# Issuing the first load of a SiLU-gate kernel as four transfers of every 8th, 4th and 2nd partition

## The chip, the cores and the metric

The kernel runs on one core of one Trainium2 chip. The metric is the device time of one execution in microseconds (us). Every run quoted here was fast, with a granted clock of 1.0. The page reckons with sixteen DMA engines (its queue lines give shares of 16 engines). Here they moved 134.22 MB from HBM into the kernel's tiles and 67.11 MB back. ACT (ScalarE) computes the SiLU and issues the loads, DVE (VectorE) does the product, and SP issues the stores.

## The reference

```python
def setup_inputs():
    batch, seq, dim = (32, 512, 2048)
    return {'x': np.random.randn(batch, seq, dim).astype(np.float32)}

def reference(x):
    half_dim = x.shape[-1] // 2
    x1, x2 = x[..., :half_dim].copy(), x[..., half_dim:].copy()
    silu_x1 = x1 * (1 / (1 + np.exp(-x1)))
    return (silu_x1 * x2).astype(np.float32)
```

134.22 MB are read and 67.11 MB are written. There is one SiLU and one product per output element, so the kernel is mostly transfer.

## The kernel before

The 16384 rows of x are cut into 16 tiles of 1024 rows. A tile is 8 MiB: 128 partitions, and in each of them 8 rows that are adjacent in HBM, which is 64 KiB. The input pool holds two tiles. A tile's store is one transfer of 4 MiB, but that of the last tile goes out in four pieces. The first load is moved ahead of the barrier at the program's start, so that it is under way as early as possible.

```python
    K = 8
    KC = 2
    PLAN = [K] * (num_rows // (P * K))
    in_pool = ctx.enter_context(tc.tile_pool(name="in_pool", bufs=2))
    out_pool = ctx.enter_context(tc.tile_pool(name="out_pool", bufs=2))
    # ... (view(flat, i) gives tile i's rows as p, k, d)
    nc.at_finalize(issue_ahead_of_the_first_barrier)   # moves the first DMA issue to before the barrier
    # ...
    def load(i):
        xt = in_pool.tile([P, K, in_cols], dt, name="xt")
        nc.scalar.dma_start(out=xt[:, :plan[i][1], :], in_=view(x_flat, i))
        loaded[i] = xt

    load(0)
    load(1)
    for i in range(n_tiles):
        # ...
        for c in range(0, k, KC):
            ce = min(c + KC, k)
            nc.scalar.activation(out=ot[:, c:ce, :], in_=xt[:, c:ce, :half],
                                 func=mybir.ActivationFunctionType.Silu)
            nc.vector.tensor_mul(out=ot[:, c:ce, :], in0=ot[:, c:ce, :], in1=xt[:, c:ce, half:])
            if last:
                nc.sync.dma_start(out=ov[:, c:ce, :], in_=ot[:, c:ce, :])
        if not last:
            nc.sync.dma_start(out=ov, in_=ot[:, :k, :])
        if i + 2 < n_tiles:
            load(i + 2)
```

## Time and profile before

| | before |
|---|---|
| time | 470.97 us (3 runs, 470.84 to 471.04) |
| span of the profiled run | 468.9 us |
| moved | 201.35 MB, mean 429 GB/s |
| DVE, ACT busy | 30%, 25% |

These lines are from the page of the kernel before. The GB/s line cuts the span into 40 slices of 11.7 us. The two queue lines give packets, MB and the packets' time as a share of sixteen engines' span; q10 carries the loads and q1 the stores. The last line gives the chain of waits as shares of the span.

```profile
DVE 142.3 (30%) x64; ACT 118.2 (25%) x65; POOL 0.2 (0%) x4
GB/s 431 375 447 403 447 447 447 403 419 431 447 447 403 447 492 363 442 492 391 458 403 439 456 447 403 409 442 447 447 403 444 467 386 447 442 419 481 400 409 354
q10 hardware_dynamic: 2304, 134.22, 66.4%
q1 hardware_dynamic: 2736, 67.11, 33.2%
DMA xt<-in_x_dram 80%; DVE ot L92 15%; ACT ot L87 3%; DVEq L128 0%
```

The two queues together fill 99.6% of the engines' span, from the first slice on. The compute engines are idle for most of it. The kernel is bound by its DMA engines, so work that is added to them anywhere is expected to show in the time.

Next is the timeline of the kernel before (start in us, duration, engine, line, operation; in brackets the idle time before it and what ended it).

```profile
0.13 1.13 ACTq L74 DMA_DIRECT2D xt<-in_x_dram  x2
1.29 1.28 ACT L87 ACT_TABLE_LOAD   x1 [1.29 <-PEq L117]
21.88 7.31 ACT L87 ACTIVATE ot<-xt 128x2048 f32<-128x2048 f32 x4 [19.31 <-DMA xt<-in_x_dram]
32.74 23.00 SPq L100 DMA_DIRECT2D out_dram<-ot  x2
44.54 7.31 ACT L87 ACTIVATE ot<-xt 128x2048 f32<-128x2048 f32 x4 [15.36 <-DMA xt<-in_x_dram]
```

Load 0 lands and releases the first activation at 21.88 us.

The stretches view counts each packet where it starts. For the first 12 us of the kernel before it gives (from:to and length in us, busy time of each engine, granted clock, DMA share, GB/s):

```profile
core 0: us, DVE busy (x) ACT busy (x) POOL busy (x), PEclk, DMA share, GB/s
0.00:4.00 4.00, 0.00 (x0) 1.28 (x1) 0.20 (x4) 1.00 0.76 262
4.00:12.00 8.00, 0.00 (x0) 0.00 (x0) 0.00 (x0) 1.00 1.21 524
```

A load packet is 64 KiB, one partition's share of a tile. 262 GB/s for 4 us is sixteen packets, 524 GB/s for 8 us is 64. The records do not name the engine of a packet. Each of the first sixteen in the order of start ends about when one of the next sixteen starts (4.37 us in the mean for both), so the k-th sixteen are called each engine's k-th packet here.

The single records behind this view give the finest reading. An engine's first packet takes 3.05 us in the mean, and each later one of load 0 takes 2.42 us in the mean, which is 27.1 GB/s for one engine.

### The profile page before, as it was taken

Reading aid. Unit: us, or ns where it says so; the run is one execution under the profiler, and the core shown is the slowest. Engines: PE = TensorE matmul, PEld = TensorE weight load, DVE = VectorE, ACT = ScalarE, POOL = GpSimd, SP = SyncE. Lnnn points to the kernel's source line nnn. Section 1 sums busy time; section 2 is a strip of 40 time slices with the busy share of each in tenths; the row PEclk is TensorE's granted clock in tenths of the full one; section 3 lists DMA queues with packets and bytes.
Section 4 is the critical chain, followed back from the end, with each engine's and each line's share of the span. In section 5 each row is a group of like instructions: output and inputs, shape, how many; then the busy total and the mean of one; then the engine's idle time right before and its main releaser. Section 6 shows DMA issues by size and latency. Waiting matters only on the chain.

```text
span 468.9 us, 269 instructions
## 1 busy us (share of the span) xinstructions
DVE 142.3 (30%) x64; ACT 118.2 (25%) x65; POOL 0.2 (0%) x4
## 2 busy tenths in 40 slices
DVE  0070705106061160601507025070250702407034
ACT  1142406023060330603206032060420604106051
POOL 0000000000000000000000000000000000000000
DMA  9899999999999998999999999999999989999998
GB/s 431 375 447 403 447 447 447 403 419 431 447 447 403 447 492 363 442 492 391 458 403 439 456 447 403 409 442 447 447 403 444 467 386 447 442 419 481 400 409 354
DMA packets 5042, 201.35 MB, mean 429 GB/s; under 512 B 560, under 2 KB 560, under 8 KB 560
## 3 DMA queue, kind: packets, MB, share of 16 engines
q10 hardware_dynamic: 2304, 134.22, 66.4%
q1 hardware_dynamic: 2736, 67.11, 33.2%
q14 instruction: 2, 0.02, 0.0%
HBM read 134.22 MB, written 67.11 MB: 429 GB/s over the span
## 4 chain that ended last, share of the span: by engine, by line
DMA 80%; DVE 15%; ACT 3%; DVEq 0%; issue 0%
DMA xt<-in_x_dram 80%; DVE ot L92 15%; ACT ot L87 3%; DVEq L128 0%
## 5 line engine op out<-in xcount | busy, mean ns | idle before, releaser
L92 DVE TENSOR_TENSOR ot<-ot,xt 128x2048 f32<-128x2048 f32 x64 | 142.3, 2286 | 319.5 <-ACT ot L87 319.5
L87 ACT ACTIVATE ot<-xt 128x2048 f32<-128x2048 f32 x64 | 116.9, 1897 | 338.8 <-DMA xt<-in_x_dram 338.8
L87 ACT ACT_TABLE_LOAD x1 | 1.3, 1283 | 1.3 <-PEq L117 1.3
L117 POOL MEMSET const-uint8-127<- 128x1 uint8 x1 | 0.1, 102 | 0.0
L117 POOL MEMSET const-bfloat16-1.0<- 128x1 bf16 x1 | 0.1, 101 | 0.0
L117 POOL MEMSET const-float32-0.0<- 128x1 f32 x1 | 0.1, 98 | 0.2 <-issue 0.2
L117 POOL MEMSET const-float32-1.0<- 128x1 f32 x1 | 0.1, 98 | 0.0
## 6 DMA issues: line engine op xcount, KB each, us to landing
out_dram<-ot SPq DMA_DIRECT2D x15, 4096.0 KB, 39.8
out_dram<-ot SPq DMA_DIRECT2D x4, 1024.0 KB, 5.7
xt<-in_x_dram ACTq DMA_DIRECT2D x16, 47.1
```

The source lines that it names most:

```text
L87: nc.scalar.activation(out=ot[:, c:ce, :], in_=xt[:, c:ce, :half], func=mybir.ActivationFunctionType.Silu,)
L92: nc.vector.tensor_mul(out=ot[:, c:ce, :], in0=ot[:, c:ce, :], in1=xt[:, c:ce, half:],)
L117: nc = _bacc.Bacc("TRN2", target_bir_lowering=False, num_devices=1)
```

## The change

The intent is a quicker start: the first transfer is small and covers every 8th partition, sixteen packets, and the transfers grow to 64 partitions. The first load alone is split. Stores stay whole, although they go through the same helper.

```diff
-def issue_ahead_of_the_first_barrier(nc):
+def issue_ahead_of_the_first_barrier(nc, count):
...
-    load = next(ins for ins in body.instructions if type(ins).__name__ == "InstDMACopy")
+    loads = [ins for ins in body.instructions if type(ins).__name__ == "InstDMACopy"][:count]
...
-    head.instructions = head.instructions[:at] + [load] + head.instructions[at:]
+    head.instructions = head.instructions[:at] + loads + head.instructions[at:]
...
+    STARTING = [slice(0, None, 8), slice(4, None, 8), slice(2, None, 4), slice(1, None, 2)]
...
-    nc.at_finalize(issue_ahead_of_the_first_barrier)
+    nc.at_finalize(lambda nc: issue_ahead_of_the_first_barrier(nc, len(STARTING)))
...
+    def start_ring(queue, dst, src, split):
+
+        for ps in STARTING if split else [slice(None)]:
+            queue.dma_start(out=dst[ps], in_=src[ps])
...
-        nc.scalar.dma_start(out=xt[:, :plan[i][1], :], in_=view(x_flat, i))
+        start_ring(nc.scalar, xt, view(x_flat, i), split=i == 0)
...
-            nc.sync.dma_start(out=ov, in_=ot[:, :k, :])
+            start_ring(nc.sync, ov, ot, split=False)
```

More of the change, by code (lines that the diff above doesn't have):

```diff
@@ L6 @@
 from concourse._compat import with_exitstack
-def issue_ahead_of_the_first_barrier(nc):
+def issue_ahead_of_the_first_barrier(nc, count):
     head, body = nc.main_func.blocks[:2]
-    load = next(ins for ins in body.instructions if type(ins).__name__ == "InstDMACopy")
+    loads = [ins for ins in body.instructions if type(ins).__name__ == "InstDMACopy"][:count]
     at = next(
         j for j, ins in enumerate(head.instructions)
-        if ins.engine == load.engine and type(ins).__name__ == "InstDrain"
+        if ins.engine == loads[0].engine and type(ins).__name__ == "InstDrain"
     )
-    body.instructions = [ins for ins in body.instructions if ins.name != load.name]
-    head.instructions = head.instructions[:at] + [load] + head.instructions[at:]
+    names = {ins.name for ins in loads}
+    body.instructions = [ins for ins in body.instructions if ins.name not in names]
+    head.instructions = head.instructions[:at] + loads + head.instructions[at:]
 @with_exitstack
```

## The prediction

> **What bounds the kernel now.** The DMA engines. On the page, load packets (66.4%) and store packets (33.2%) fill 99.6% of the sixteen engines' span of 468.9 us; DVE is busy 30%, ACT 25%. The chain of waits is 80% loads of xt. In the trace's DMA records every load packet is 64 KiB (one partition's row of a tile) and takes 2.418 us, 27.1 GB/s per engine, from each engine's second packet on. 201.35 MB at sixteen times that rate is 464.2 us (estimate), so only 4.7 us of the span are not transfer: 1.14 us before the first packet (in the stretches view no bytes in the first microsecond, sixteen packets start in the second), first packets of 3.0 to 3.4 us, two engines that start 0.6 us after the others, and the tail after the last load.
>
> **What the change does.** The first 8 MiB load becomes four issues. A DMA issue costs ACT 0.33 to 0.38 us, so three more are about 1 us; they delay load 1's issue and the activation table load, both of which have until about 20 us. No cost. The possible gain is a quicker start with a short first transfer: 0.1 to 0.3 us, since nothing before the first issue moves. 48 more completion packets of 9 ns, three per engine: nothing. Computation waits for the whole tile as before.
>
> **The cost I expect.** [...] So in the first two transfers [...] each 1 MiB should take about 4.84 us instead of 2.42. [...] Estimated loss: 2 x 2.42 = 4.84 us[...], less the start gain: 4 us net.
>
> **On the critical path?** Wholly. Load 1 is queued behind load 0 and the queues never run empty before the end, so transfer time lost at the start moves everything; nothing later takes it up.
>
> **Prediction.** 474.8 us, about 0.8% slower; 80% range 470.8 to 476.0. Chances: faster by over 2% 0.005, within 2% 0.955, slower by over 2% 0.04.
>
> **What would show it.** Load queue 2352 packets (2304 + 48). Each engine's first two packets take 4.5 to 5.3 us, the third onward 2.42. The first activation starts near 26 us instead of 21.88; all later steps come 4 us later at unchanged distances (58 us per two tiles). ACT and DVE busy unchanged.
>
> **What would make it wrong.** [...] Slow reads of rows 512 KiB apart would look alike[...].

Passages are cut from this text and from some of the expectations below, where the cuts are marked: they rested on statements of the hardware that no trace or run here shows. The sum of the forecast came to a loss of about 4 us: 2 x 2.42 = 4.84 us, less a term of 0.2 to 0.6 us, less the gain of 0.1 to 0.3 us at the start. The 2.42 us was measured in the kernel before. That the packets of the two 16-partition transfers take twice as long was the estimate; no trace had shown it then.

## The result, and the profile after

The changed kernel takes 475.0 us (6 runs, 474.89 to 475.18), beside 471.0 us for the kernel before (6 runs, 470.71 to 471.12). The ratio is 1.0086, with a 95% interval of 1.0073 to 1.0099. It is a slowdown of 0.9%, clear of noise but within 2%. Ratios in this document are the mean time of one kernel's fast runs over that of the other's fast runs of the same rounds, so they are not quite the ratio of the medians quoted.

The same lines of the page, for the changed kernel (slices of 11.8 us):

```profile
DVE 142.3 (30%) x64; ACT 118.2 (25%) x65; POOL 0.2 (0%) x4
GB/s 244 377 443 443 427 460 443 399 438 449 402 441 443 471 416 399 443 488 399 410 477 443 399 419 429 438 444 460 410 460 399 441 446 443 399 443 482 380 425 354
q10 hardware_dynamic: 2352, 134.22, 66.6%
q1 hardware_dynamic: 2736, 67.11, 32.9%
DMA xt<-in_x_dram 79%; DVE ot L101 15%; ACT ot L96 3%; DVEq L137 0%; ACTq L96 0%
```

Only the first slice stands out: 244 GB/s in place of 431. Compute is the same to the digit. The load queue has 48 packets more: in the DMA records it has 304 packets of 4 bytes in place of 256, of 9 ns each and sixteen to each transfer, and there are three transfers more.

The timeline and the first stretches of the changed kernel:

```profile
0.13 3.54 ACTq L77 DMA_DIRECT2D xt<-in_x_dram  x5
27.34 1.28 ACT L96 ACT_TABLE_LOAD   x1 [27.34 <-DMA xt<-in_x_dram]
28.63 7.31 ACT L96 ACTIVATE ot<-xt 128x2048 f32<-128x2048 f32 x4
39.50 20.77 SPq L77 DMA_DIRECT2D out_dram<-ot  x2
49.06 7.31 ACT L96 ACTIVATE ot<-xt 128x2048 f32<-128x2048 f32 x4 [13.12 <-DMA xt<-in_x_dram]
```

```profile
0.00:4.00 4.00, 0.00 (x0) 0.00 (x0) 0.20 (x4) 1.00 1.19 262
4.00:12.00 8.00, 0.00 (x0) 0.00 (x0) 0.00 (x0) 1.00 0.96 254
```

From 4 to 12 us the engines start two packets each (one of the 32 falls just outside) where they started four before. The DMA share stays near 1 (0.96): the engines are not waiting for work. Each of the first two packets simply takes about twice as long (4.77 and 4.95 us, below). Also, the activation table is now loaded after the wait for load 0 instead of at 1.29 us. The second tile's activation is 4.52 us late (49.06 against 44.54), and the span is 4.2 us longer (473.1 against 468.9).

The DMA records give the sixteen packets of each step of load 0, one per engine, as the mean in us:

| | before | changed |
|---|---|---|
| start of the first packet | 1.32 (1.14 to 1.84) | 1.76 (1.50 to 2.60) |
| 1st packet takes | 3.05 | 4.77 (4.24 to 5.27) |
| 2nd packet | 2.42 | 4.95 (4.95 to 4.96) |
| 3rd packet | 2.42 | 2.86 (2.60 to 3.13) |
| 4th to 8th packet, each | 2.42 | 2.42 |
| 8th packet ends | 21.28 | 26.43 |

The slow packets are the first two of each engine, the ones of the two 16-partition transfers. The sixteen of the first transfer are in flight together: the last starts at 2.60 us, and none has ended by then, since the shortest takes 4.24 us from 1.50 us at the earliest. (The steps here are the packets in order of their start, sixteen at a time.)

### The profile page after: what moved, and what is told of

It is laid out like the page before. It is cut to its first block, busy times and chain, and to the rows that moved or that the text cites. A ratio compares the mean times of both kernels' runs of the same rounds, so it can differ in the third digit from the quotient of the medians.

```text
span 473.1 us, 277 instructions
## 1 busy us (share of the span) xinstructions
DVE 142.3 (30%) x64; ACT 118.2 (25%) x65; POOL 0.2 (0%) x4
## 4 chain that ended last, share of the span: by engine, by line
DMA 79%; DVE 15%; ACT 3%; DVEq 0%; issue 0%; ACTq 0%
DMA xt<-in_x_dram 79%; DVE ot L101 15%; ACT ot L96 3%; DVEq L137 0%; ACTq L96 0%
```

## The experiments

The theory is that the set of partitions that a transfer writes sets the time of its packets; in the changed kernel it is 4.77 and 4.95 us for every 8th and 2.42 us for every 2nd. Why a set should be slow is not shown by any trace here. The theory's forecast is the one that stands before those of the rivals. The rivals are: several transfers or several issues cost by themselves; small transfers do; HBM rows that lie 512 KiB apart (every 8th partition, 64 KiB each) are slow to read; the queues are slow only while they start up. The first four runs share the kernel before at 470.78 us (9 runs), the next four at 470.92 us (11 runs), the last three at 470.86 us (7 runs).

### Three transfers of 32, 32 and 64 partitions

```diff
-    STARTING = [slice(0, None, 8), slice(4, None, 8), slice(2, None, 4), slice(1, None, 2)]
+    STARTING = [slice(0, None, 4), slice(2, None, 4), slice(1, None, 2)]
```

> First load as three transfers of every 4th and 2nd partition (32, 32, 64): the change without its two 16-partition transfers, [...] from each engine's second packet on 2.42 us; time 471.0 to 471.4 (the start may be 0.4 us later, as in the changed kernel). Rival 'several transfers cost': loss falls only with their number, about 473.5 to 474.

Measured: 471.81 us (5 runs, 471.60 to 472.82), ratio 1.0025 (1.0013 to 1.0038). Every packet of load 0 from the second on takes 2.42 us, and load 0's 8th packets end at 21.70 us. Merging the two 16-partition transfers into one of 32 removes nearly all of the loss. What remains, 1.0 us, is above the expected range. In the trace it is 0.42 us from the start and about 0.5 us from a stall at the first store, which a later section takes up. Even without slow packets after the first the split start is slower than the whole one (471.81 us against 470.78).

### Four transfers of 32 partitions

```diff
+    STARTING = [slice(0, None, 4), slice(2, None, 4), slice(1, None, 4), slice(3, None, 4)]
```

> Four transfers as in the change, but 32 partitions each (every 4th, offsets 0, 2, 1, 3). [...] 471.0 to 471.4, packets 2.42 us from the second on. Rival 'four issues at the start cost': 475.

Measured: 471.83 us (4 runs, 471.48 to 472.27), ratio 1.0021 (1.0008 to 1.0035). The packets take 2.42 to 2.43 us from the second on. Four issues ahead of the barrier cost no more than three (471.83 us against 471.81), so the number of transfers isn't the cause.

### The same four sizes, contiguous

```diff
+    STARTING = [slice(0, 16), slice(16, 32), slice(32, 64), slice(64, 128)]
```

> Same four sizes 16, 16, 32, 64, but contiguous partitions (0-15, 16-31, 32-63, 64-127), rows packed too. [...] loss near 28 us, time 496 to 501. Rival 'rows read 512 KiB apart are slow': rows are 64 KiB apart, so no loss, 471. Rival 'small transfers': 475 as the change.

Measured: 499.46 us (4 runs, 499.06 to 499.54), ratio 1.0605 (1.0589 to 1.0621). This is the GB/s line of its page (slices of 12.4 us):

```profile
GB/s 169 105 232 169 421 463 390 453 421 463 421 421 463 406 437 421 463 421 421 463 421 421 421 463 422 421 463 417 427 424 461 421 421 463 416 427 429 456 419 340
```

Four slow slices stand where the changed kernel has one. The 1st and 2nd packets, those of the two transfers of sixteen contiguous partitions, take 8.61 and 9.35 us; the 4th to 8th, into 32 and 64 contiguous ones, take 4.98 to 5.12 us. The loss of 28.7 us is near the 28 of the forecast. Here the source rows are adjacent, and the sizes are the same as in the change. Neither the rival of distant rows nor that of small transfers allows it.

### The change's partitions, from adjacent source rows

```diff
+    ROWS = [slice(0, 16), slice(16, 32), slice(32, 64), slice(64, 128)]
...
-        for ps in STARTING if split else [slice(None)]:
-            queue.dma_start(out=dst[ps], in_=src[ps])
+        for ps, rs in zip(STARTING, ROWS) if split else [(slice(None), slice(None))]:
+            queue.dma_start(out=dst[ps], in_=src[rs])
```

> Destination partitions as in the change, but the source rows of each transfer adjacent (0-15, 16-31, 32-63, 64-127), so the first tile's rows are permuted and the result is wrong on purpose. [...] 475.0 as the change, first two packets of each engine about 4.8 and 4.95 us. Rival 'rows 512 KiB apart are slow to read': 471.

Measured: 475.13 us (4 runs, 474.94 to 475.29), ratio 1.0091 (1.0077 to 1.0105), and the result is wrong. The first two packets take 4.83 and 4.91 us (4.77 and 4.95 in the changed kernel). The distance between the source rows has nothing to do with the slow packets. For these reads of 64 KiB rows no run here shows a loss by pitch (475.0 us from rows 512 KiB apart, 475.13 from adjacent ones). But rows 512 KiB apart were read only in the slow packets (4.77 us and more); at 2.42 us a packet the runs have rows 256 KiB apart (every 4th partition).

### The four transfers in the opposite order

```diff
+    STARTING = [slice(1, None, 2), slice(2, None, 4), slice(4, None, 8), slice(0, None, 8)]
```

> The change's four transfers in the opposite order (64, 32, 16, 16)[...] each engine's first packet about 3.1 us, its 7th and 8th 4.5 to 5 us each; load 0's packets end near 26.8 us; time 474.9 to 475.6. Rival 'short transfers hurt only while the queues start up': 471.5 to 472.5.

Measured: 475.46 us (4 runs, 475.41 to 475.88), ratio 1.0098 (1.0085 to 1.0111). First packets take 3.21 us, the 7th and 8th take 4.72 and 4.90 us, and load 0's packets end at 26.56 us. The loss goes with the two 16-partition transfers, at the load's end as at its start. It isn't an effect of the start.

### The activation table early

```diff
     load(0)
     load(1)
+    warm = ctx.enter_context(tc.tile_pool(name="warm", bufs=1)).tile([P, 1], dt, name="warm")
+    nc.vector.memset(warm, 0.0)
+    nc.scalar.activation(out=warm, in_=warm, func=mybir.ActivationFunctionType.Silu)
```

> The changed kernel with a 128x1 activation right after the two load issues, which brings the activation table in early. In the changed kernel the table load waits for load 0 and the first activation is at 28.63 us. Theory 'off the critical path': first activation at about 27.35 us, first store 1.3 us earlier, time 474.7 to 475.2. Rival 'the table load adds its 1.28 us': 473.7.

Measured: 475.02 us (4 runs, 474.97 to 475.12), ratio 1.0087 (1.0074 to 1.0100), the same as the changed kernel's 475.0 us and 1.0086. From the timeline of this run:

```profile
3.70 1.28 ACT L90 ACT_TABLE_LOAD   x1 [3.70 <-PEq L129]
27.60 7.31 ACT L99 ACTIVATE ot<-xt 128x2048 f32<-128x2048 f32 x4 [22.40 <-DMA xt<-in_x_dram]
38.46 0.37 SPq L77 DMA_DIRECT2D out_dram<-ot  x1
```

The first activation comes 1.03 us earlier than in the changed kernel (27.60 against 28.63), and the first store as well (38.46 against 39.50); the forecast was 27.35 and 1.3 us. The time does not move. The late table load, conspicuous as it is in the profile, costs nothing, because load 1 keeps the DMA engines busy meanwhile (a DMA share of 0.91 from 20 to 28 us).

### A later first store, in the kernel before

The traces held something that no theory had asked for. In the kernel before, the load packet of each engine that precedes its first store packet takes 3.2 to 3.4 us (it starts near 35.7 us). Over all load packets around the first store this makes 0.90 us per engine; in the runs with 32-32-64 and with four of 32 it is 1.4 us. In the changed kernel no packet there is slow (0.01 us). Its first store goes out later, so the first idea was that the time of the first store decides.

```diff
     load(1)
+    idle = ctx.enter_context(tc.tile_pool(name="idle", bufs=1)).tile([P, 2048], dt, name="idle")
+    nc.vector.memset(idle, 0.0)
...
+            for _ in range(1 if i == 0 and c == KC else 0):     # 4 in the second kernel
+                nc.scalar.activation(out=idle, in_=idle, func=mybir.ActivationFunctionType.Silu)
```

> The kernel before with one dummy 1.9 us activation in the first tile, so that the first store is issued near 34.2 us instead of 32.7, as in the three-transfer run. In the traces of before[...], the load packets of all engines were slow for some time at 36 to 41 us (0.9 to 1.3 us lost in the mean of the engines); in the changed kernel, whose first store goes out at 39.5, none was. Theory 'the first store's time decides': stall remains, 470.8 to 471.8. Rival 'only the changed kernel's load pattern avoids it': the same here.

> The same with four dummy activations: the first store is issued near 40 us, as late as in the changed kernel. Theory 'the first store's time decides': no stall near 36 to 41 us, time 470.0 to 470.3. Rival 'the stall comes with the first store whenever it is issued': stall moves to 42 to 46 us, time 470.8 to 471.1. Rival 'a late store costs by itself': above 471.1.

With one dummy: 471.24 us (5 runs, 471.01 to 471.90), ratio 1.0009 (0.9997 to 1.0021); first store issued at 34.42 us, stall of 1.19 us on packets that start at 38.1 to 38.7 us. With four: 473.13 us (6 runs, 472.24 to 476.63), ratio 1.0062 (1.0036 to 1.0087); first store issued at 40.33 us, stall of 1.37 us on packets that start at 41.3 to 42.6 us. The stall follows the first store, although that store was issued even later than the changed kernel's. The idea that its time decides is wrong. The time of the second kernel fits none of these theories but the third, that a late store costs by itself (above 471.1), and cannot be put down to it: the dummies also delay the issue of load 2 to 40.33 us, when load 1 is nearly in (it lands at 41.52), so the engines stand empty for 0.9 us between 40 and 43 us, and the runs scatter.

### The four transfers in load 1

```diff
-        start_ring(nc.scalar, xt, view(x_flat, i), split=i == 0)
+        start_ring(nc.scalar, xt, view(x_flat, i), split=i == 1)
...
-    nc.at_finalize(lambda nc: issue_ahead_of_the_first_barrier(nc, len(STARTING)))
+    nc.at_finalize(lambda nc: issue_ahead_of_the_first_barrier(nc, 1))
```

> Load 0 whole as in the kernel before; the four transfers (16, 16, 32, 64) are made of load 1 instead. [...] first packets start at 1.14 us again and the first activation is at 21.9 to 22.2 us; each engine's 9th and 10th packets take 4.8 to 5.0 us. Second question, the stall of all engines at the first store, [...] no load packet slow at the first store, time 474.7 to 475.3. Rival 'it is the kernel with a split first load that avoids it': stall of 0.9 to 1.4 us there, 475.7 to 476.4.

The first of the two theories was that the stall at the first store goes away when the slow transfers come before that store, in whichever load.

Measured: 476.22 us (4 runs, 476.15 to 476.28), ratio 1.0111 (1.0094 to 1.0128). The slow packets are where the transfers were put: the 9th, 10th and 11th packets take 4.65, 4.94 and 2.87 us. The stall is gone, as the first theory said; no load packet after those is slow. Yet the time is 0.9 us above that theory's range and within the rival's. The trace shows where it went: engines without a packet in the last 20 us of the span (counted up to the last packet of all) make 1.45 us per engine, against 0.56 us in the kernel before. About 1.3 us of it lie between 461.3 and 463.3 us, around the first store of the last tile, which is issued at 462.21 us; the kernel before has no such gap before its last packets. Three stretches of 10 us at the end show the same gap, first in this run, then in the kernel before (9 us in its last line):

```profile
445.00:455.00 10.00, 0.00 (x0) 0.00 (x0) 0.00 (x0) 1.00 0.99 429
455.00:465.00 10.00, 5.11 (x3) 7.05 (x4) 0.00 (x0) 1.00 0.82 347
465.00:475.00 10.00, 3.78 (x2) 0.26 (x1) 0.00 (x0) 1.00 0.81 334
```

```profile
440.00:450.00 10.00, 0.00 (x0) 0.00 (x0) 0.00 (x0) 1.00 1.05 452
450.00:460.00 10.00, 7.03 (x4) 7.31 (x4) 0.00 (x0) 1.00 0.95 407
460.00:469.00 9.00, 1.86 (x1) 0.00 (x0) 0.00 (x0) 1.00 0.77 327
```

The middle stretch, in which the last tile is computed, is the one to look at: a DMA share of 0.82 against 0.95, so the engines stand empty for longer there. Moving one load's landing has probably changed what is still queued at the end; that was not tested, and the forecast had not reckoned with it. Two smaller misses belong to this run. The 9th packets were forecast at 4.8 us or more. And the first activation was at 23.10 us, later than forecast: load 0's last 4-byte packets are through at 21.80 us, much as in the next run (21.83), but it counts as landed only 1.28 us later, against 0.35 us there. Why stays open.

### The four transfers in load 5

```diff
+        start_ring(nc.scalar, xt, view(x_flat, i), split=i == 5)     # else as in load 1
```

> The four transfers are made of load 5, in the middle of mixed load and store traffic, all else as before. [...] still slower than before, by 1 to 5 us[...], 472 to 476; first activation at 21.9 to 22.2 us. [...] Rival 'only a loss at the very start is on the critical path': 471.

Measured: 476.61 us (4 runs, 476.40 to 476.84), ratio 1.0120 (1.0105 to 1.0135), a little above the range. The 41st and 42nd load packets take 4.50 and 4.58 us, so in the middle of mixed traffic the slow packets cost 4.2 us per engine on load packets, nearly what they cost at the start (4.69 us). Some of the store packets between them are slow as well (up to 1.46 us instead of 1.21), which is another 0.3 us per engine. The stall at the first store is there (1.1 us on packets near 36 us), as it should be if only slow transfers before that store remove it. The end has 1.19 us of empty engines, 0.6 us more than before.

### Two halves

```diff
+    STARTING = [slice(0, 64), slice(64, 128)]
```

> First load as two transfers of 64 contiguous partitions (0-63, 64-127)[...] all 8 packets of each engine in load 0 take about 5 us, load 0's packets end near 41.8 us instead of 21.5, time 489.5 to 491.5. Rival 'only transfers of 16 partitions are slow': 471 to 471.5.

Measured: 491.42 us (4 runs, 491.31 to 491.60), ratio 1.0434 (1.0419 to 1.0450), within the forecast. The GB/s line of its page (slices of 12.2 us):

```profile
GB/s 257 171 171 343 466 428 391 434 460 404 468 423 428 460 391 434 423 452 447 428 434 460 391 466 429 450 439 402 428 460 402 428 463 420 460 399 436 428 428 343
```

The 2nd to 8th packets take 4.95 to 5.12 us each, and load 0's packets end at 42.25 us. The most natural split of a load into two is five times as costly as the change. It costs 20.6 us for one 8 MiB load. The number of transfers does not account for that: three or four in a row cost 1.0 us above. What the trace shows is packets of twice the length.

## Why the prediction was right

**The cost was right; its mechanism is not shown.** The prediction took the packets of the two 16-partition transfers to be twice as long, which was the author's estimate. The runs agree, and the packet time goes with the set of partitions in each of them:

| partitions of one transfer | us a packet, means of sixteen | runs |
|---|---|---|
| every 2nd or every 4th | 2.42 from the 2nd packet on | three transfers, four of 32 |
| every 8th | 4.65 to 4.95 | the change, its opposite order, adjacent rows, load 1 |
| every 8th, among stores | 4.5 to 4.6 | load 5 |
| 32 or 64 contiguous | 4.95 to 5.12 (4th to 8th packet; 2nd to 8th) | contiguous; halves |
| 16 contiguous | 8.61 (1st packet), 9.35 (2nd) | contiguous |

The records do not name the engine of a packet, so which engines slow each other, and where, is not shown. What is shown is that the slowing goes with the set of partitions, not with number, size, place or source of the transfers. Other sets of sixteen were not run, so it is not shown that a transfer of that size can keep 2.42 us.

**On the critical path was right in kind.** Load 0's packets end 5.15 us later (26.43 against 21.28), and 4.2 us of it are in the span. Apart from the stall below, the engines have almost no free time into which the loss could go: in the kernel before, the two queues fill 99.6% of their span.

**The sum was right, its terms less so.** This is the difference of the two spans, in us per engine, from the DMA records:

| term | predicted | measured |
|---|---|---|
| start of the first packets | -0.1 to -0.3 | +0.44 |
| first three packets: 12.58 against 7.89 | +4.2 to +4.6 | +4.69 |
| stall at the first store: 0.01 against 0.90 | none | -0.89 |
| engines empty in the last 20 us, up to the last packet: 0.44 against 0.56 | none | -0.12 |
| not assigned | | +0.11 |
| span | about +4 | +4.23 |

- "The possible gain is a quicker start with a short first transfer: 0.1 to 0.3 us" failed. The first packets start 0.44 us later. The issue of the first transfer takes 0.59 us instead of 0.38 (the trace's DMA issues), where the prediction had 0.33 to 0.38 us for every issue. That is about half of the delay. With the strided transfers of 32 or 64 partitions in front, the first issue takes 0.55 to 0.57 us and the start is late too; with sixteen contiguous partitions it takes 0.39 us and the first packet starts at 1.17 us. A stride is not needed for a long issue: the first of the halves, 64 contiguous partitions, takes 0.54 us, and its earliest packet starts at 1.47 us. So the late start goes with the long issue, whose cause stays open, and a small transfer earns nothing. Some engines start late in every variant (the last first packet starts at 1.84 us in the kernel before, at 2.60 in the changed one).
- "The third onward 2.42" failed for the third: 2.86 us. The same 2.8 to 2.9 us appears in load 1's first packets after the opposite order (2.89) and after the halves (2.88). It is not there in load 5 (the 43rd packets take 2.42 us), where store packets lie between. The engines that arrive earliest have the longest, 3.13 us, and the last has 2.60 us: 0.53 us less for a start 1.07 us later. Neither that nor the 0.18 us that even the last has above 2.42 is settled.
- "The first activation starts near 26 us" failed: 28.63 us. Of the 6.75 us, 5.15 are load 0, 1.28 the table load, now behind the wait for the load, and the rest a slightly slower landing. The prediction said the table load had time until 20 us; it did not see that the load would be placed after that wait. The run with an early table shows that this costs nothing in the end.
- "Nothing later takes it up" failed by about 0.9 us: the stall at the first store, which the kernel before has, is missing. It is in all six traces of kernels without slow transfers before their first store (0.9 to 1.4 us: before, 32-32-64, four of 32, one and four dummies, the four transfers in load 5) and in none of the six with them in load 0 (changed, contiguous, adjacent rows, opposite order, early table, halves), nor in that with them in load 1. How they take the stall away stays open. That it is not a matter of the time of the first store is shown by the dummies; that it goes with whether slow transfers came before that store, by loads 1 and 5.

So 474.8 us came as close to 475.0 as it did partly by luck: a start that was 0.5 to 0.7 us worse than forecast and a stall that vanished cancelled each other. The part that made the slowdown, the slow packets, was 4.69 us against 4.2 to 4.6.

No version here is faster than the kernel before. The whole load issued first remains the best start that was tried.

## What to carry to other kernels

Look at the set of partitions that each single transfer covers, not only at its bytes: on this kernel, whose DMA engines are full (99.6%), packets of a transfer to every 8th partition or to a contiguous half took about twice as long (4.5 to 5.12 us against 2.42), and the loss appeared in the total in each of the three loads where the four transfers were tried (0, 1 and 5: 475.0, 476.22 and 476.61 us against 470.86 to 471.0). If a load has to be split by partition, take every 2nd or every 4th, which here kept 2.42 us a packet; the sets of sixteen that were tried and a contiguous half did not. And a prediction that hits the total should still be checked term by term, since two wrong terms can cancel.

## What else the traces show

- In the halves run, the 2nd to 8th packets take 4.95 to 5.12 us, most of them 5.12, with the engines busy (8 or 9 tenths in each slice of the page): 16 x 65536 bytes in 5.12 us is 205 GB/s (212 in 4.95). That is slightly more than twice the 2.418 us of the kernel before (4.84 us). The 9.35 us of the second sixteen contiguous partitions is not more than four times that (9.67 us).
- An issue took 0.33 to 0.38 us for the whole tile (kernel before), 0.39 to 0.44 us for 16 or 32 contiguous partitions (contiguous run), 0.54 to 0.61 us for 64 contiguous ones (halves and contiguous runs), and 0.55 to 0.62 us for every 8th, 4th or 2nd (changed kernel, three transfers).
- Reads of 64 KiB rows 512 KiB apart lost nothing here (475.0 us, against 475.13 us from adjacent rows), though only in the slow packets; rows 256 KiB apart were read at the full 2.42 us a packet (four of 32).
